# Shifting a matrix by halves with DMAs alone: which two quarters of the columns one DMA takes

## The chip, the cores and the metric

The kernel runs on one core of a Trainium2 chip. The metric is the device time of one execution in microseconds (us), and the time given for a kernel is the median over several runs. A separate execution is taken with the hardware profiler; its page and its trace are what this document reads.

A core has 16 DMA engines that move data between places in memory. The compute engines (TensorE, VectorE, ScalarE, GpSimd, which the profile calls PE, DVE, ACT and POOL) play no part in this kernel. SyncE (SP) issues the DMAs: one instruction describes a whole transfer by two access patterns, for the source and for the destination, and the transfer is then cut into packets that the DMA engines work off.

## The reference

The input is a float32 matrix of 8192 x 8192 (268 MB); the output is the same matrix shifted by half its size in both directions, cyclically:

```
def reference(x: np.ndarray) -> np.ndarray:
    return np.fft.ifftshift(x)
```

With R = C = 8192, `out[i, j] = x[(i + 4096) % 8192, (j + 4096) % 8192]`. Nothing is computed. Every element is read once and written once.

A row has 32,768 bytes. In what follows a row is thought of as four quarters of 2,048 columns (8,192 bytes), Q0 to Q3. Quarter q of an output row is quarter (q + 2) mod 4 of the input row that lies 4,096 rows away: Q0 comes from Q2, Q1 from Q3, Q2 from Q0 and Q3 from Q1.

## The kernel before, in words

Both matrices lie in the device's main memory (the profile calls it HBM; the tensors are `in_x_dram` and `out_dram`). The kernel copies straight from one to the other, with nothing in between, in a double loop (lines 37 to 42): `apart` is 4, `rows` is 16 x 4 = 64, `piece` is a quarter, 2,048 columns. The outer loop goes over 128 blocks of 64 rows. The inner loop issues two DMAs for each block, 256 in all, every one on SP's queue (`nc.sync`).

The helper `both` (lines 25 to 34) builds a DMA. Its destination pattern has three dimensions: 64 rows at a step of a row, 2 pieces at a step of half a row (`hc`), and 2,048 columns in succession. Its source pattern has the same shape, begins in the other half of the row, and steps back by half a row between the two pieces. So the first DMA of a block (`col` = 0; called A below) writes Q0 and Q2 of each of its 64 rows, reading Q2 and Q0; the second one (`col` = `piece`; called B) writes Q1 and Q3, reading Q3 and Q1. A DMA moves 64 x 2 pieces of 8,192 bytes, 1 MB.

The pieces of a DMA are spread over the 16 DMA engines, eight to each, and each engine adds a small packet that reports that its share is done. The order of the issues is the order of the loop. Nothing in the kernel waits for data; the framework gives the DMAs eight completion semaphores in rotation, so that an issue waits for the DMA that was issued eight before it.

Of the kernel before, what the change touches and what calls it, by code (L numbers as in the profile page):

```python
# [1 line left out]

# [4 lines left out]


ENGINES = 16  # L10


@with_exitstack
def kernel(
    ctx: ExitStack,
    tc: tile.TileContext,
    x: bass.AP,
    out: bass.AP,
):
    nc = tc.nc  # L20
    R, C = x.shape
    hr = R // 2
    hc = C // 2

    def both(queue, row, col, rows, piece):

        queue.dma_start(
            out=bass.AP(out.tensor, out.offset + row * C + col, [[C, rows], [hc, 2], [1, piece]]),
            in_=bass.AP(
                x.tensor,  # L30
                x.offset + (row + hr) % R * C + hc + col,
                [[C, rows], [-hc, 2], [1, piece]],
            ),
        )


    apart = 4
    piece = hc // 2
    rows = ENGINES * apart
    for row in range(0, R, rows):  # L40
        for col in (0, piece):
            both(nc.sync, row, col, rows, piece)


# [1 line left out]
_INS = ['x']  # L46
_OUTS = [((8192, 8192), 'float32')]


def kernel(**inputs):  # L50
    import numpy as _np
    import concourse.bacc as _bacc
    import concourse.tile as _tile
    from concourse import mybir as _mybir
    from concourse.bass_utils import run_bass_kernel_spmd as _run

    nc = _bacc.Bacc("TRN2", target_bir_lowering=False, num_devices=1)  # L57
    arrays, args = {}, []
    for name in _INS:
        a = _np.ascontiguousarray(inputs[name])  # L60
        if a.dtype.kind in "iu":
            a = a.astype(_np.int64)
        arrays[f"in_{name}_dram"] = a
        args.append(nc.dram_tensor(f"in_{name}_dram", a.shape, _mybir.dt.from_np(a.dtype), kind="ExternalInput").ap())
    for i, (shape, dtype) in enumerate(_OUTS):
        dt = _mybir.dt.from_np(_np.dtype(dtype))
        args.append(nc.dram_tensor(f"out_{i}_dram", shape, dt, kind="ExternalOutput").ap())
    with _tile.TileContext(nc) as tc:
        kernel(tc, *args)
    r = _run(nc, [arrays], core_ids=[0])  # L70
    got = tuple(r.results[0][f"out_{i}_dram"] for i in range(len(_OUTS)))
    return got[0]
```

## Time and profile before

| | |
|---|---|
| time, median of 3 runs (lowest, highest) | 811.06 us (810.09, 811.13) |
| the profiled execution's own time | 810.44 us |
| its span, first to last instruction | 808.7 us |
| DMAs issued, size of each | 256, 1024 KB |
| median time from issue to landing | 25.1 us |
| bytes moved by the DMA engines, mean rate | 268.47 MB, 332 GB/s |
| share of the span in which SP's DMA queue kept the 16 engines busy | 99.3% |

How to read it: the page has six parts. The first is the busy time of the engines (here only POOL's four settings of constants, 0.2 us). The second cuts the span into 40 equal slices and gives, for each, the busy share of the DMA engines in tenths (9 is 90% or more) and the rate. The third is a table of DMA queues: packets, megabytes, and the time that the packets took as a share of the span of 16 engines. The fourth is the chain of waits that ended last, the fifth lists groups of instructions, and the sixth the DMA issues by line, with the time from issue to landing. Line 27 (L27) is the `queue.dma_start` in the helper. The trace behind the page holds a record for every packet: when it started, how long it took, and how many bytes it had. "GB/s" counts a copied byte once; the line that begins with HBM counts it twice, as read and as written.

### The profile page before, as it was taken

To read this page: it belongs to the slowest core of one execution; us is meant where nothing else is said; L and a number is where in the kernel's file an instruction comes from. 1 tells how busy PE (TensorE), PEld (TensorE's weight loads), DVE (VectorE), ACT (ScalarE), POOL (GpSimd) and SP (SyncE) were. 2 spreads that over 40 slices of the span, in tenths; PEclk is the share of its full clock that TensorE was granted. 3 is DMA by queue.
4 is the path that set the end of the run, shared out by engine and by line. 5 is a ranking of instruction groups with operands and counts; after the bars stand their busy time and mean duration, and the time that the engine had idled before them with its cause. 6 is when DMAs were issued, how large, how long until landed. Compare 5 with 4: busy or idle time off the path is not lost. (4 is left out here: it accounts for less than half of the span.)

```text
span 808.7 us, 301 instructions
## 1 busy us (share of the span) xinstructions
POOL 0.2 (0%) x4
## 2 busy tenths in 40 slices
POOL 0000000000000000000000000000000000000000
DMA  8999999999999999999999999999999999999998
GB/s 301 331 335 329 336 334 330 335 332 336 332 335 334 336 331 334 339 328 335 331 335 339 334 334 337 331 336 330 336 334 331 339 332 334 333 336 331 337 335 294
DMA packets 36866, 268.47 MB, mean 332 GB/s; under 512 B 4096, under 2 KB 4096, under 8 KB 4096
## 3 DMA queue, kind: packets, MB, share of 16 engines
q1 hardware_dynamic: 36864, 268.45, 99.3%
q14 instruction: 2, 0.02, 0.0%
HBM read 268.44 MB, written 268.44 MB: 664 GB/s over the span
## 5 line engine op out<-in xcount | busy, mean ns | idle before, releaser
L57 POOL MEMSET const-bfloat16-1.0<- 128x1 bf16 x1 | 0.1, 102 | 0.0
L57 POOL MEMSET const-uint8-127<- 128x1 uint8 x1 | 0.1, 102 | 0.0
L57 POOL MEMSET const-float32-1.0<- 128x1 f32 x1 | 0.1, 99 | 0.0
L57 POOL MEMSET const-float32-0.0<- 128x1 f32 x1 | 0.1, 98 | 0.2 <-issue 0.2
## 6 DMA issues: line engine op xcount, KB each, us to landing
out_dram<-in_x_dram SPq DMA_DIRECT2D x256, 1024.0 KB, 25.1
```

What stands on the lines that cost most here:

```text
L57: nc = _bacc.Bacc("TRN2", target_bir_lowering=False, num_devices=1)
```

## The change

The helper takes the first column of each of its two pieces instead of one column and a fixed step of half a row. The loop over `col` is replaced by two calls. The number, the size and the queue of the DMAs are those of before.

```
-    def both(queue, row, col, rows, piece):
+    def two(queue, row, first, second, rows, piece):
 
+        source = (first + hc) % C
+        there = second - first
+        back = (second + hc) % C - source
         queue.dma_start(
-            out=bass.AP(out.tensor, out.offset + row * C + col, [[C, rows], [hc, 2], [1, piece]]),
+            out=bass.AP(
+                out.tensor,
+                out.offset + row * C + first,
+                [[C, rows], [there, 2], [1, piece]],
+            ),
             in_=bass.AP(
                 x.tensor,
-                x.offset + (row + hr) % R * C + hc + col,
-                [[C, rows], [-hc, 2], [1, piece]],
+                x.offset + (row + hr) % R * C + source,
+                [[C, rows], [back, 2], [1, piece]],
             ),
         )
...
     for row in range(0, R, rows):
-        for col in (0, piece):
-            both(nc.sync, row, col, rows, piece)
+        two(nc.sync, row, 0, hc + piece, rows, piece)
+        two(nc.sync, row, hc, piece, rows, piece)
```

The first DMA of a block now writes Q0 and Q3 (a step of 24 KB) and reads Q2 and Q1 (a step of 8 KB back). The second writes Q2 and Q1 (8 KB back) and reads Q0 and Q3 (24 KB forward).

## The prediction

> **What bounds the kernel now.** I read the page from its DMA parts outward, since no compute engine does anything: the queue table and the memory line first, then the 40 slices, the chain, the wait list of SP's own queue, and last the separate packet records of the trace.
>
> The queue table (queue, kind, packets, megabytes, share of sixteen engines' span) and the memory line under it:
>
> ```profile
> DMA packets 36866, 268.47 MB, mean 332 GB/s; under 512 B 4096, under 2 KB 4096, under 8 KB 4096
> ## 3 DMA queue, kind: packets, MB, share of 16 engines
> q1 hardware_dynamic: 36864, 268.45, 99.3%
> q14 instruction: 2, 0.02, 0.0%
> HBM read 268.44 MB, written 268.44 MB: 664 GB/s over the span
> ```
>
> The sixteen DMA engines are busy 99.3% of the span: there is no idle time to win, only the length of a packet. The packets are 32,768 of 8,192 bytes with data (256 DMAs x 128) and 4,096 small ones that report completion (16 for each DMA).
>
> ```profile
> DMA  8999999999999999999999999999999999999998
> GB/s 301 331 335 329 336 334 330 335 332 336 332 335 334 336 331 334 339 328 335 331 335 339 334 334 337 331 336 330 336 334 331 339 332 334 333 336 331 337 335 294
> ```
>
> The rate is flat. Between the first and the last slice it stays within 328 and 339, and those two are the ramp and the drain. There is no stage that is worse than another.
>
> The chain of waits holds nothing of use: its seven pieces end after half a microsecond with POOL's constants, so it doesn't follow the transfers. The list of waits of SP's queue does:
>
> ```profile
> engine line waited for: us in total, times, longest us
> SPq L27 <- DMA out_dram<-in_x_dram: 634.0, 248, 3.2
> SPq L68 <- DMA out_dram<-in_x_dram: 24.1, 4, 15.2
> ```
>
> and the row of the issues, by tensor:
>
> ```profile
> L27 SPq DMA_DIRECT2D out_dram<-in_x_dram x256: 562/562/682, 0.7 to 783.1; - x128
> DMA to landing us min/median/max: 6.0/25.1/26.0
> ```
>
> An issue takes SP 562 ns; 248 of the 256 issues (all but eight) first wait for an earlier DMA to land, 634.0 / 248 = 2.56 us each. 808.7 / 256 = 3.16 us pass per DMA, so a landing time of 25.1 us means eight DMAs in flight. SP is ahead of the engines throughout.
>
> What a packet costs I took from the single packet records. The 8,192-byte ones take 391.0 ns on average, the completion packets 9 ns. Check: (32,768 x 391.0 + 4,096 x 9) / 16 = 803.1 us, which is the 99.3% of 808.7. The durations have a floor: 62% of the data packets take 307 to 320 ns, the median is 309, and the other 38% reach up to 1,507. So 391.0 is 309 plus a mean stall of 82 ns. [...] That is the only thing that this change can reach. The conversion for all that follows: each engine moves 32,768 / 16 = 2,048 data packets, so **1 ns per data packet is 2.05 us**, and 0.2% of the time (1.6 us, about what a measurement of this kernel can tell from no change) is 0.8 ns per packet.
>
> **The change, part by part.** Call the four 8 KB quarters of a 32 KB row Q0 to Q3. Output quarter q always comes from input quarter q+2 (mod 4) of the row 4,096 rows away. Before, DMA A writes Q0,Q2 (reads Q2,Q0) of 64 rows and DMA B writes Q1,Q3 (reads Q3,Q1). After, A writes Q0,Q3 (reads Q2,Q1) and B writes Q2,Q1 (reads Q0,Q3).
>
> *Counts, sizes, issue.* 256 DMAs of 64 x 2 x 8 KB, one queue, one wait each: all as before; the access patterns keep their three dimensions, and one with a negative step stands in every DMA of before too (input side). So 256 x 562 ns = 144 us of SP's issue time stay, covered by the 2.56 us wait each. An issue would have to grow from 562 ns to over 3.1 us to show. Cost 0. The start (first issue at 0.7 us) and the drain (last slice at 294 GB/s) have the same DMA sizes: 0.
>
> *Packets.* The same 32,768 of 8,192 bytes. In the new order two neighbours in an engine's sequence can be contiguous in memory (Q3 of a row, then Q0 of the next), but they are separate runs of the pattern, so I count no merging. Cost 0.
>
> *Order of addresses.* This is all that is left, and the trace of before shows no run with the new order, so I bound it. I chained the packet records per engine (each next packet starts 3 to 4 ns before the end of the one before it; 3,131 sequences between two completion packets come out unambiguous, 76% of all). That gives the mean duration by place in the engine's eight packets (four rows of two pieces; I take it that the rows of an engine follow each other): 400.6, 386.2, 389.4, 398.0, 401.9, 384.7, 390.0, 401.7 ns, each +-2.6, mean 394.1. Three things are read from it.
>
> First, reads against writes. Before, every second packet of an engine reads the same row offset that the packet before it wrote, and writes the one that it read (places 1, 3, 5, 7, counting from 0). After, no quarter is both read and written within a DMA. If such meetings cost anything, odd places would be dearer than even ones. They are 393 against 395: nothing to win there.
>
> Second, mixing. Before, all packets of one DMA stand in even quarters or all in odd ones; other engines' packets are of the other kind only around a change of DMA. After, each DMA holds both kinds, half and half. The trace has this mixture at the two places beside the change of DMA (0 and 7, where 0.375 of the overlapping packets belong to another DMA), and, without it, at the two places beside the middle of a DMA (3 and 4, where that share is 0.05), which otherwise look alike, since the engines step to the next pair of rows there too. Means: 401.15 against 399.95, a difference of +1.2 +- 2.7 ns. The mixture's share there is 0.325 more; the change raises it over all packets from 0.17 (mean of the eight places) to 0.5, as much. So the direct estimate is +1.2 +- 2.7 ns, +2.5 +- 5.5 us: not told from zero.
>
> Third, the ends. Four places (1, 2, 5, 6) average 387.6, the four others 400.6: the largest effect of place on a packet that before shows, 6.5 ns to either side of the mean. If the new order made all packets like the cheap places, 6.5 x 2.05 = 13 us would go (798); if like the dear ones, 13 us would come (824). I take 0, since the two comparisons that bear on this change (393/395 and 401/400) show nothing, and keep 798 and 824 for the range.
>
> A fourth row agrees: in the first 20 us the engines run within about 1 us of each other (spread of the sixteen completions of a DMA), later within 2 to 2.5 us, so that quarters go from nearly in step to well mixed; the full slices at the start (331 335 329 336) and the end (331 337 335) are the same.
>
> Sum: 810.44 us of the profiled execution + 0 = 810.4, and the median of the three runs, 811.06, lies 0.6 above it. I forecast **811 us**, no change.
>
> A rule of the skill, beside this sum: the Trainium skill, DMA: Bandwidth & Descriptors, Latency and other measured facts, reports that copies between memory tensors slow down when parallel streams lie at large powers of two (207 GB/s at a 512 KiB pitch, 103 at 4 MiB, and 214 again with 4 KiB of padding) and infers, unverified, that lock-stepped streams fall on the same channels. The engines here step by powers of two, so by that rule breaking the common 16 KB step would help; the trace's flat rate from in-step to mixed speaks against its applying to this bit. And the Trainium skill, HBM Reference, Specifications, gives about 716 GB/s per domain: the row's 664 would be 93% of that, and 536.9 MB at 716 an estimate of 750 us, so by that page little could be won however the order is changed.
>
> **The rivals.** *Slower: the leader pays for mixed quarters.* An engine that enters a new DMA while the others are still in the old one stalls more. At place 0 with over 0.6 of its neighbours in the other DMA the mean is 453 ns; at place 4 with over 0.6 of them in the other half of the same DMA it is 432. The 20.6 ns between them, at a share of about 0.8, could be the price of meeting the other kind of quarter. Raised by 0.33 for all packets this is 8.5 ns, 17 us, 828; laggards show none of it (place 7 against place 3: both about 399), so with half of the packets leading it is 4.2 ns, 9 us: 820. Against it: the means over leaders and laggards. It decides from 0.8 ns per packet on.
>
> *Faster: reads and writes in separate quarters.* Within a DMA all reads go to two quarters and all writes to the other two. If memory keeps a quarter's rows open for one direction, packets come out like the cheap places: 387.6, 798 us. For it: cheap and dear places exist at all, so some address pattern matters. Against it: odd places read just what was written before them and are no dearer. This is also where the page's rule on pitches would lead.
>
> *The transfer changes kind:* the pattern is cut into other packets, or the rows spread over the engines otherwise. Nothing in the rows speaks for it; both patterns keep 64 rows outermost. I give it no time of its own, and 0.02 within the slower case.
>
> **How the numbers follow.** No effect of order: 0.44, of which 0.27 within 0.2%, 0.08 faster and 0.09 slower, as 0.8 ns per packet is a third of the uncertainty of my comparison. Leader pays: 0.32 at about 820 (813 to 828). Separate quarters: 0.24 at about 798 (790 to 806). So faster 0.32, within 0.2% 0.27, slower 0.41. The range 799 to 824 holds the first case (0.44), three quarters of the second (0.24) and half of the third (0.12), together 0.80; the first case's own range is 806 to 816.
>
> **What would show it.** Right: 36,864 packets on q1, DMA share about 99.3%, slices between 328 and 339, 562 ns an issue, about 25.1 us to landing, a mean data packet of 391 +- 1 ns with 62% at the floor. The slower rival: same floor, fewer packets at it, mean near 395, slices near 328, landing near 25.4. The faster one: mean near 385, slices near 338, HBM line near 674. Wrong altogether: another number of packets, or a floor that moves.

## The result and the profile after

The changed kernel takes 815.94 us (median of 9 runs, 813.66 to 820.76), the kernel before, beside it, 811.83 us (9 runs, 810.09 to 813.65). The ratio is 1.0056 with a 95% interval from 1.0031 to 1.0080: slower by about half a per cent, 4.1 us. The forecast was no change at 811; the loss lies inside the range that was given, but the interval leaves no change out.

The profiled execution is one of the longer ones, 819.08 us with a span of 817.3 us, so its own difference to the profile of before (8.6 us) is twice that of the medians. From the page of the changed kernel, the DMA parts:

```profile
GB/s 293 328 316 321 321 331 329 330 332 335 333 334 334 334 329 335 327 326 329 333 330 324 331 333 332 338 325 329 344 331 331 335 330 328 330 331 339 333 330 284
DMA packets 36866, 268.47 MB, mean 328 GB/s; under 512 B 4096, under 2 KB 4096, under 8 KB 4096
q1 hardware_dynamic: 36864, 268.45, 99.3%
HBM read 268.44 MB, written 268.44 MB: 657 GB/s over the span
out_dram<-in_x_dram SPq DMA_DIRECT2D x256, 1024.0 KB, 25.3
```

The packets are the same in number and size and the engines are as busy as before; only the rate is lower, 328 for 332 GB/s. An issue takes 573 ns instead of 562, and SP still waits before 248 of them (from the row of the issues and the wait list of the changed kernel):

```profile
L30 SPq DMA_DIRECT2D out_dram<-in_x_dram x256: 572/573/693, 0.7 to 791.8; - x128
SPq L30 <- DMA out_dram<-in_x_dram: 640.2, 248, 3.9
```

The 11 ns per issue are covered by 2.58 us of waiting each (640.2 / 248). In the packet records the mean of a data packet is 395.1 ns, for 391.0 before: 4.1 ns x 2.05 us = 8.4 us, nearly the whole difference of the two spans (8.6). The floor is where it was (median 309 ns), and more packets are at it than before, 65.9% for 61.8%. So fewer packets stall, but those that do stall longer.

Where in time it is lost, the slices show first at the beginning: 316, 321, 321 in the third to fifth, where before had 335, 329, 336. Busy time in stretches (start and end, length, POOL's busy time and count, TensorE clock, DMA share, GB/s), before:

```profile
0.00:40.00 40.00, 0.20 (x4) 1.00 0.95 316
40.00:80.00 40.00, 0.00 (x0) 1.00 1.00 331
80.00:160.00 80.00, 0.00 (x0) 1.00 1.00 334
160.00:320.00 160.00, 0.00 (x0) 1.00 1.00 335
320.00:480.00 160.00, 0.00 (x0) 1.00 1.00 334
480.00:640.00 160.00, 0.00 (x0) 1.00 1.00 334
640.00:800.00 160.00, 0.00 (x0) 1.00 1.00 334
```

and after:

```profile
0.00:40.00 40.00, 0.20 (x4) 1.00 0.95 310
40.00:80.00 40.00, 0.00 (x0) 1.00 0.99 319
80.00:160.00 80.00, 0.00 (x0) 1.00 1.00 328
160.00:320.00 160.00, 0.00 (x0) 1.00 1.00 333
320.00:480.00 160.00, 0.00 (x0) 1.00 1.00 329
480.00:640.00 160.00, 0.00 (x0) 1.00 1.00 333
640.00:800.00 160.00, 0.00 (x0) 1.00 1.00 332
```

The new order is 3.6% slower from 40 to 80 us (319 against 331) and 0.3 to 1.5% slower after 160 us. By the missing GB/s times the length of each stretch, the first 160 us hold 240 + 480 + 480 = 1,200 GB/s x us, which at 332 GB/s is 3.6 us. The 640 us after them hold 320 + 800 + 160 + 320 = 1,600, or 4.8 us. So the loss is densest at the beginning, but in this long execution more than half of it comes later. The profiles below show the first part each time, and the second not always.

### The profile page after: what moved, and what is told of

The parts are those of the page before. It is cut to its first block, busy times and chain, and to the rows that moved or that the text cites. A ratio compares the mean times of both kernels' runs of the same rounds, so it can differ in the third digit from the quotient of the medians.

```text
span 817.3 us, 301 instructions
## 1 busy us (share of the span) xinstructions
POOL 0.2 (0%) x4
## 2 busy tenths in 40 slices
DMA packets 36866, 268.47 MB, mean 328 GB/s; under 512 B 4096, under 2 KB 4096, under 8 KB 4096
```

## The experiments

All ratios are against the kernel before on the same chip; chips differ (811 us on some, 823 on one), so across chips only ratios are compared. The diffs are against the changed kernel. "Spread" below is the time from the first to the last of the sixteen completions of one DMA, and "step" the time from one DMA's median completion to the next one's, both from the landing records; they tell how far the engines stand apart and how fast they are. "Near step" means a small spread.

### Which part of the order costs

The changed kernel once more, without an edit, beside three other orders.

> The changed kernel once more, beside the kernel before on one chip, for the size of the loss and for a second profile. All theories: ratio to before near 1.005 (1.003 to 1.008). The first profile lost most in the first 80 us (310 and 319 GB/s in the two windows of 40 us, against 316 and 331 before) and about 0.7% later; if this is the change and not that one execution, the second profile shows it again: under 325 GB/s in the window from 40 to 80 us.

Measured: 825.62 us against 823.25, ratio 1.0037 (1.0021 to 1.0053). The dip is there again: 305 and 322 GB/s in the first two stretches of 40 us, 328 to 330 after. The kernel with the order turned in DMA B (below), which is as fast as before on this chip, has 312 and 329, then 328 to 329. So this profiled execution, the shortest of its nine (824.39 us), loses nothing after 80 us.

Neighbouring quarters:

```
-        two(nc.sync, row, 0, hc + piece, rows, piece)
-        two(nc.sync, row, hc, piece, rows, piece)
+        two(nc.sync, row, 0, piece, rows, piece)
+        two(nc.sync, row, hc, hc + piece, rows, piece)
```

> DMA A writes Q0,Q1 (reads Q2,Q3), DMA B writes Q2,Q3 (reads Q0,Q1): neighbours, 16 KB contiguous, ascending on both sides. As in the changed kernel, both 8 KB parities are in flight within a DMA and no quarter is both read and written. Theory 1, mixing both parities costs: slower by 0.3 to 0.8%, 814 to 818 us. Theory 2, reads and writes in separate quarters cost (or the kernel before gains by touching the same row offset for both): slower by as much. Theory 3, the descending writes of DMA B cost: no descending here, so 811 to 813, as before. Theory 4, the pairing of outer with inner quarters itself (steps of 24 and 8 KB by turns): 811 to 813.

Measured: 1.0022 (1.0009 to 1.0034). But this kernel changed something else too, as the packet line of its page shows:

```profile
DMA packets 20482, 268.47 MB, mean 326 GB/s; under 512 B 4096, under 2 KB 4096, under 8 KB 4096
```

Without the 4,096 completion packets and the two instruction packets these are 16,384 packets with data, of 16 KB: two pieces that lie in succession on both sides travel as one. So the run doesn't decide between the theories. It does have the dip (308 and 322 GB/s in the first two stretches of 40 us) without any descending order, which speaks against theory 3.

The pairs of before with the order turned in DMA B:

```
-        two(nc.sync, row, 0, hc + piece, rows, piece)
-        two(nc.sync, row, hc, piece, rows, piece)
+        two(nc.sync, row, 0, hc, rows, piece)
+        two(nc.sync, row, hc + piece, piece, rows, piece)
```

> The pairs of the kernel before, but DMA B writes Q3 first and then Q1 (reads Q1, then Q3): only the order within DMA B is turned, writes descend there. Theories 1, 2 and 4: as before, 811 to 813, ratio within 0.2%. Theory 3 (descending writes in DMA B, or turning the order from DMA to DMA): slower by 0.3 to 0.8%.

Measured: 1.0002 (0.9994 to 1.0011), as before.

The new pairs with DMA B ascending:

```
-        two(nc.sync, row, hc, piece, rows, piece)
+        two(nc.sync, row, piece, hc, rows, piece)
```

> The pairs of the changed kernel (Q0,Q3 and Q1,Q2), but DMA B writes Q1 first and then Q2, ascending (reads Q3, then Q0). Theory 3: the loss is gone, 811 to 813. Theories 1, 2 and 4: still slower by 0.3 to 0.8%, 814 to 818.

Measured: 1.0030 (1.0014 to 1.0047). Theory 3, the descending order, falls by both runs: turning alone costs nothing, and unturning doesn't help. The loss is in which quarters a DMA pairs.

Neighbours again, descending, so that they aren't merged:

```
-        two(nc.sync, row, 0, hc + piece, rows, piece)
-        two(nc.sync, row, hc, piece, rows, piece)
+        two(nc.sync, row, piece, 0, rows, piece)
+        two(nc.sync, row, hc + piece, hc, rows, piece)
```

> DMA A writes Q1 then Q0 (reads Q3, Q2), DMA B writes Q3 then Q2 (reads Q1, Q0). The earlier run with neighbours in ascending order moved 16 KB packets (16,384 of them), since the two pieces were contiguous; descending, they stay apart, 32,768 packets of 8 KB expected. So it has both parities in flight and separate quarters for reads and writes, with another pairing than the changed kernel. Theories 1 and 2 (mixing, separate quarters): slower by 0.3 to 0.5%. Theory 4 (the pairing of outer with inner quarters): as before, within 0.2%.

Measured: 816.93 us against 810.98, 1.0067 (1.0043 to 1.0091), somewhat more than the 0.3 to 0.5% expected, with 32,768 data packets of 8 KB as expected and the dip (310 and 321 GB/s, then 327, 328 and from 160 us on 333 to 335). Theory 4 falls: it is not the pairing of outer with inner quarters.

One quarter per DMA (`one` is a helper like `two` with a single piece; its definition is left out here):

```
-        two(nc.sync, row, 0, hc + piece, rows, piece)
-        two(nc.sync, row, hc, piece, rows, piece)
+        for col in (0, hc, piece, hc + piece):
+            one(nc.sync, row, col, rows, piece)
```

> One quarter per DMA: 512 DMAs of 64 x 8 KB in the order Q0, Q2, Q1, Q3, so that reads and writes stand in separate quarters within a DMA, but only one parity is in flight. It has 4,096 more completion packets (9 ns each, 2.3 us, 0.28%) and twice the issues (512 x 0.57 = 292 us, covered). Theory 1 (mixing parities): 1.003 from the completion packets alone. Theory 2 (separate quarters): 1.006 to 1.008.

Measured: 813.39 against 810.98, 1.0032 (1.0022 to 1.0042): the price of the completion packets, with no dip (its stretch from 40 to 80 us is at 334 GB/s). So reads and writes in separate quarters cost nothing by themselves. What the three slow orders with 8 KB packets (the changed kernel, DMA B ascending, neighbours descending) have in common, and the three others (before, order turned, single quarter) lack, is that a DMA touches all four quarters, even and odd ones together. Even and odd quarters together without the separation of reads and writes would need a pattern of four dimensions in one DMA and wasn't tried, so it is not shown that the mixing alone, without the separation, would cost as much.

### When it costs

The new pairs for 16 blocks only, at the beginning, and the reverse:

```
     for row in range(0, R, rows):
-        two(nc.sync, row, 0, hc + piece, rows, piece)
-        two(nc.sync, row, hc, piece, rows, piece)
+        if row < 16 * rows:
+            two(nc.sync, row, 0, hc + piece, rows, piece)
+            two(nc.sync, row, hc, piece, rows, piece)
+        else:
+            two(nc.sync, row, 0, hc, rows, piece)
+            two(nc.sync, row, piece, hc + piece, rows, piece)
```

> The new pairs for the first 16 of the 128 blocks (32 DMAs, about the first 100 us, in which the profiles of the changed kernel lose most), the pairs of before for the other 112. Theory S (the loss is in the start, while the sixteen engines run nearly in step): the whole loss remains, ratio to before 1.003 to 1.005. Theory E (every block loses the same): an eighth of it, ratio 1.0005, not told from 1.

> The reverse: the pairs of before for the first 16 blocks, the new pairs for the other 112. Theory S: no loss, ratio 0.998 to 1.001 (it could even gain, as the windows after 160 us of the second profile of the changed kernel are 1 GB/s above those of the kernel with the order turned in DMA B). Theory E: seven eighths of the loss, 1.003 to 1.004.

Measured: 1.0036 (1.0023 to 1.0049) with the new order in an eighth of the blocks, and 1.0032 (1.0020 to 1.0044) with it in the other seven eighths. Neither theory had both. The loss does not go with the number of blocks (theory E falls), and it is not tied to the beginning of the kernel (theory S falls). The stretches of the first, new until about 100 us:

```profile
40.00:80.00 40.00, 0.00 (x0) 1.00 0.99 324
80.00:120.00 40.00, 0.00 (x0) 1.00 1.00 324
120.00:160.00 40.00, 0.00 (x0) 1.00 0.99 336
```

and of the second, new from about 100 us:

```profile
40.00:80.00 40.00, 0.00 (x0) 1.00 1.00 326
80.00:120.00 40.00, 0.00 (x0) 1.00 1.00 334
120.00:160.00 40.00, 0.00 (x0) 1.00 0.99 326
160.00:320.00 160.00, 0.00 (x0) 1.00 0.99 332
```

In the first run the dip goes away together with the new order (324, then 336). In the second one the rate falls where the new order begins and recovers while it stays (326, then 332). That second dip is weak evidence by itself: the same run has one stretch of 326 with the old pairs too, from 40 to 80 us. The time is the firmer part: all five executions took 813.5 us or more, against 810.98.

Spread and step, medians and means over 16 DMAs, with the beginning of the new order marked by `>`:

```
DMAs             0-15         16-31        32-47        64-79        128-143      144-159
                 spread step  (us, ns)
before           1.1  3124    1.1  3148    1.1  3153    1.4  3125    2.1  3145    2.1  3116
changed        > 1.3  3223    1.3  3262    2.1  3161    2.7  3163    3.4  3178    3.4  3158
new first      > 1.2  3236    1.2  3256    1.3  3122    1.2  3134    1.4  3134    1.6  3152
old first        1.2  3170    1.1  3133  > 1.5  3189    1.7  3160    2.2  3136    2.2  3146
four spells    > 1.2  3193    1.3  3230    1.8  3180    2.1  3155  > 2.2  3162    2.2  3165
old half first   1.1  3108    0.9  3155    1.1  3140    1.2  3141  > 1.5  3185    1.4  3169
half new       > 1.3  3237    1.5  3233    1.7  3275    2.2  3178    -     -      -     -
changed, again > 1.2  3253    1.3  3222    1.2  3238    1.6  3178    1.9  3134    2.1  3137
```

The last four rows belong to the next experiments ("changed, again" is the changed kernel beside the staggered ones). Over the sixteen groups of the kernel before, the step lies between 3,112 and 3,172 ns, so a single value under about 3,180 tells little. What the table suggests is that the new order is slow while the engines stand within about 1.5 us of each other. It is no sharp line (3,275 at 1.7 us), and it is not the whole loss of the first profile, which had its stretch of 329 GB/s at a spread of about 3.3 us.

### Is it a time to settle, or the engines being near step

Four spells: new for blocks 0 to 31 and 64 to 95, the pairs of before for the others (`if row // (32 * rows) % 2 == 0` in the diff above). Old half first: the pairs of before for `row < R // 2`, then the new ones.

> Blocks 0 to 31 with the new pairs, 32 to 63 with those of before, 64 to 95 new, 96 to 127 before: the new order is entered twice. Theory T (a settling time: each time the new order begins, the first 32 to 64 DMAs run 1 to 3% slower, about 3 us in all, and after that the two orders run at the same rate): twice the loss, ratio 1.006 to 1.008, and a dip in the rate at the start and again at about 404 us. Theory T1 (a settling time at the start of the kernel alone, or only while the engines are within 1.5 us of each other): the loss of one entry, 1.003 to 1.004, no dip at 404 us. Theory E (every block of the new order loses the same): half of the loss of the changed kernel, 1.002.

> The first 64 blocks with the pairs of before, the other 64 with the new ones. By the switch, at about 404 us, the completions of the sixteen engines are some 2 us apart, not 1.2 as at the start. Theory T: the whole loss, 1.003 to 1.004, with the dip after the switch. Theory T1 (engines near step are what the new order can't bear): no loss, 0.999 to 1.001. Theory E: half, 1.002, with no dip.

Measured: four spells 1.0056 (1.0043 to 1.0068), old half first 1.0022 (1.0012 to 1.0031). Four spells in stretches, the new order entered again at about 404 us:

```profile
40.00:100.00 60.00, 0.00 (x0) 1.00 1.00 326
300.00:400.00 100.00, 0.00 (x0) 1.00 1.00 333
400.00:440.00 40.00, 0.00 (x0) 1.00 1.00 332
440.00:500.00 60.00, 0.00 (x0) 1.00 1.00 333
```

and old half first, entered at about 404 us for the first time:

```profile
300.00:400.00 100.00, 0.00 (x0) 1.00 1.00 334
400.00:440.00 40.00, 0.00 (x0) 1.00 1.00 329
440.00:500.00 60.00, 0.00 (x0) 1.00 1.00 329
500.00:600.00 100.00, 0.00 (x0) 1.00 1.00 332
```

The profile of four spells has no second dip, which fits T1; the time of 1.0056 is above T1's one entry, and below T's two. Old half first has a dip, which fits T, but there the spread hadn't reached the 2 us that I expected: it was 1.2 us up to the switch. Both profiles agree with a loss near step only. The times leave it undecided.

Only the first 64 blocks, with the new pairs and with those of before (`range(0, R // 2, rows)`; both leave out the lower half of the output):

> The changed kernel, but only the first 64 blocks: it leaves out the lower half of the output. To be held against the next run, which does the same with the pairs of before. Theory T: the loss is a fixed one and stays near 3 us (2 to 4) at half the length. Theory E: it halves, to 1.5 us or so.

> The kernel before, but only the first 64 blocks: it leaves out the lower half of the output. About 0.502 of the whole kernel's time, 407 us on a chip where that takes 811, as the ramp and the drain stay. The run before this one is longer by 2 to 4 us under theory T, by 1.5 us under theory E.

Measured: 415.82 us (412.73 to 418.64) against 408.58 (408.14 to 409.40), 7.2 us. Not the 2 to 4 of theory T, but certainly not the half of theory E: at half the length the loss is no smaller than over the whole matrix (4.1 us on the first chip). So most of it belongs to the time after the order begins. In the profile of this run that time is longer than in the first one: 305, 325 and 324 GB/s up to 200 us, where the half with the old pairs has 318, 333 and 333.

### Trying to set the engines apart, and bringing them back

The engines dealt apart in the first block: 48 of its 64 rows go as before, the last 16 in small DMAs of unequal length (`one` again without its definition):

```
+    level = 3 * ENGINES
+    two(nc.sync, 0, 0, hc + piece, level, piece)
+    two(nc.sync, 0, hc, piece, level, piece)
+    for quarter, some in enumerate((12, 11, 10, 9)):
+        one(nc.sync, level, quarter * piece, some, piece)
+        one(nc.sync, level + some, quarter * piece, ENGINES - some, piece)
-    for row in range(0, R, rows):
+    for row in range(rows, R, rows):
```

> The changed kernel, but in the first block the last 16 rows are dealt out in eight small DMAs of one quarter each (12 and 4 rows, 11 and 5, 10 and 6, 9 and 7), so that, if a DMA of n rows goes to the first n engines, the sixteen engines begin the second block up to 8 packets (about 3 us) apart instead of in step. All of the matrix is copied. The engine with the most work has 4 packets above the mean, some 1.5 us at the end. Theory T1 (near step is what costs): no dip, 331 to 335 GB/s in the window from 40 to 100 us, and within 1 us of the staggered kernel of before. Theory T (settling, whatever the spread): the dip remains, 319 to 327 GB/s, and the time lies 2 to 4 us above the staggered kernel of before.

> The same stagger with the pairs of before: what the stagger itself costs. Both theories: 0 to 2 us above the kernel before (ratio 1.000 to 1.0025), no dip.

> The changed kernel on the same chip as the two staggered ones, for the size of its loss there. Both theories: ratio 1.003 to 1.008, with the dip.

Measured on one chip, before at 810.58: the changed kernel 816.82, 1.0069 (1.0051 to 1.0087), with the dip (306 and 324 GB/s up to 100 us); staggered with the old pairs 812.55, 1.0019 (1.0011 to 1.0028), as expected; staggered with the new pairs 819.80, 1.0112 (1.0084 to 1.0140). The loss of the new order against the old one with the same stagger is 7.3 us. It fits neither theory: T1 had no loss, T had a dip of 100 us, and this one lasts, at least in the profiled execution, which is the longest of its six (824.45 us). New pairs, staggered:

```profile
40.00:100.00 60.00, 0.00 (x0) 1.00 1.00 327
200.00:300.00 100.00, 0.00 (x0) 1.00 1.00 327
700.00:800.00 100.00, 0.00 (x0) 1.00 1.00 330
```

Old pairs, staggered:

```profile
40.00:100.00 60.00, 0.00 (x0) 1.00 1.00 333
700.00:800.00 100.00, 0.00 (x0) 1.00 1.00 334
```

The stagger didn't do what it was meant to do. The landing records put the spread, medians of 16 DMAs, at 1.6 to 1.9 us in the first 128 whole DMAs of the new order and at 1.1 to 1.7 in those of the old, not at the 3 us of the dealing: the engines had come nearly together again by the first whole DMA (0.6 and 0.8 us). So a wide spread from the start was not tried. What the pair does show is that one threshold for the spread is not enough: with the new pairs the step stayed at 3,161 to 3,207 ns, 3,183 on average, where the spread was 1.9 to 2.2 us, while the second new spell of four spells and the changed kernel in two profiles had 3,134 to 3,167, 3,151 on average, at 1.9 to 2.2. T1 in its plain form falls by this. That two executions with the same spread have the engines in different arrangements, and that the new order minds which one, would explain it, but no record here tells one arrangement from another. The old pairs, staggered, run at 332 to 334 from 40 to 800 us.

The changed kernel beside them supports the part of T1 that is left. In this execution the spread stayed at 1.2 to 1.3 us for the first 64 DMAs, twice as long as in the first profile, and the dip lasted about twice as long too: 324 and 325 GB/s up to 200 us, 330 in the next 100 us, then 333 to 335 to the end, as fast as the old pairs. What was left to ask is whether being near step causes the dip, or only the beginning of something.

Brought back into step seven times (`seen` is a tile of 16 x 8; its two lines are left out here):

```
     for row in range(0, R, rows):
         two(nc.sync, row, 0, hc + piece, rows, piece)
         two(nc.sync, row, hc, piece, rows, piece)
+        if row // rows % 16 == 15 and row + rows < R:
+            nc.sync.dma_start(out=seen[:, :], in_=bass.AP(out.tensor, out.offset + (row + rows - 16) * C + piece, [[C, 16], [1, 8]]))
+            nc.sync.dma_start(out=bass.AP(out.tensor, out.offset + (row + rows - 16) * C + piece, [[C, 16], [1, 8]]), in_=seen[:, :])
```

> The changed kernel, but after every 16 blocks (32 DMAs) SP reads back 16 short pieces of what the last DMA wrote, and writes the same values to the same place, before it issues the next block. So the engines run empty seven times and begin in step again eight times in all. Theory P (the dip comes from the engines being in step, a bad arrangement for four quarters): each of the eight spells of about 100 us runs 1 to 3% slower than with the old order, 2 to 3 us each, together 12 to 25 us above the next run. Rival B (the dip belongs to the beginning of the kernel, or to a change of order): once 3 to 5 us, as without the drains.

> The same seven drains with the pairs of before: what the drains cost by themselves, an estimated 25 to 60 us (each one lets the engines run empty for two round trips of short DMAs and then fill up; the shortest landing time in the trace of before is 6.0 us). Theory P: the run before this one is 12 to 25 us longer; rival B: 3 to 5 us.

Measured, before at 811.24: new 835.44 (832.87 to 836.13), ratio 1.0289 (1.0272 to 1.0306); old 815.18 (813.61 to 816.45), ratio 1.0045 (1.0032 to 1.0058). The difference is 20.3 us, in the upper half of theory P; rival B had 3 to 5. My estimate of the drains' own cost, 25 to 60 us, was far too high: with the old pairs they took about 4 us. The engines did not run empty as planned, either. The trace shows the first DMA of the next block issued ahead of the read, and the second one between the read and the write, so the DMAs in flight fall from eight to one or two. In the packet records all sixteen engines stand still together at only one of the fourteen drains. That was enough to keep them near step. Stretches of the new order:

```profile
300.00:400.00 100.00, 0.00 (x0) 1.00 1.00 322
400.00:500.00 100.00, 0.00 (x0) 1.00 0.99 323
600.00:700.00 100.00, 0.00 (x0) 1.00 0.99 323
```

and of the old one:

```profile
300.00:400.00 100.00, 0.00 (x0) 1.00 1.00 332
600.00:700.00 100.00, 0.00 (x0) 1.00 1.00 333
```

The dip of the first 100 us is now the whole run. In both kernels the spread stays at 1.1 to 1.9 us to the end, where the undrained ones reach 2.4 and 3.4; away from the drains the mean step is 3,228 ns with the new pairs and 3,141 with the old, 2.8% apart (87 ns x 256 DMAs = 22 us; the two spans are 21.8 us apart). Most of it is not in the drains themselves: the mean data packet is 400.2 ns against 391.4, and 8.8 ns x 2.05 us = 18.0 us of the 21.8. So at the same spread, with the same drains, the new order is the slower one, and kept near step it stays slow.

## Why the prediction was wrong

**What bounds the kernel, the parts that stay, the conversion:** right. Packets, floor, queue share and cover of the issues came out as told, and 2.05 us per ns accounts for nearly all of the difference of the two spans. The issue was not quite "as before" (573 for 562 ns), without effect.

**Reads against writes, "nothing to win there":** right, and confirmed from the other side: single quarters, with reads and writes apart, gain nothing and lose nothing beyond their completion packets.

**Mixing, "the direct estimate is +1.2 +- 2.7 ns, +2.5 +- 5.5 us":** the measured loss of 4.1 us is 2.0 ns per packet and lies within it. I set this term to 0 because it could not be told from zero; but zero had to be within 0.8 ns, and the comparison couldn't tell that. The best value that I had was on the slow side. That it comes near is luck, though: the four places on which it rests went down in the changed kernel (401.2 to 394.3 and 399.8 to 397.7 ns), and others went up.

**The ends, "I take 0":** here the change shows in the records. Chained as in the prediction, those of the changed kernel give 1,898 unambiguous sequences, with 395, 393, 391, 385, 410, 403, 401 and 394 ns by place, each +-3. The four places that were cheap (387.6) now take 396.9 ns, the four that were dear (400.6) take 396.0. With the drains it is the same, only more: from the old pairs to the new ones the cheap places go from 380.7 to 404.7 ns, the dear ones from 407.5 to 402.1. The new order loses the cheap places. The two comparisons that set this term to 0 could not see that: they held dear places against dear ones, or averaged cheap and dear.

**The step that failed is the 0 for the order of addresses,** which measured 2.0 ns per packet by the medians. Its last support was the fourth row, "the engines run within about 1 us of each other ... later within 2 to 2.5 us, so that quarters go from nearly in step to well mixed; the full slices ... are the same". The reading is true for the old order and was carried over to the new one. The old order is indifferent to how the engines stand (near step, drifted, after the stagger, drained: 330 to 335 GB/s in every stretch of 100 us or more after the start, on the chips where it takes 811 us), the new one is not: 322 to 326 kept near step, 327 to 330 after the stagger, 329 to 335 when drifted. A trace of a kernel that is insensitive to something can't price it for one that is sensitive.

**The rivals.** "The leader pays" had the direction and most of its signs (mean near 395, landing near 25.4, HBM line below 664), but told fewer packets at the floor, and there were more; its price of 9 us was spread evenly over the run, while the measured loss is densest where the engines are near step. Nor do the places agree with it: 3 and 4, where the share of neighbours of the other kind was lowest before (0.05) and so had most to gain, went from 399.8 to 397.7 ns, not up. "Separate quarters" as a gain is refuted. The Trainium skill, DMA: Bandwidth & Descriptors, Latency and other measured facts, infers that lock-stepped streams at large powers of two collide. That being near step matters to the new order is shown here (3,228 ns per DMA kept near step, 3,151 on average at a spread of about 2 us), but the orders that broke the common 16 KB step, which I took to help by that rule, are the ones that are sensitive to it; the order that kept it is not.

**What stays open:** why an order that touches all four quarters in a DMA is slower near step than one that touches two, and whether the mixing or the separation that comes with it does it. Which addresses collide, if any do, which arrangement is a good one, and why the run after the stagger stayed slow, no run here shows. Nor is it shown why the first profile lost 4.8 us after 160 us with the engines well apart, while two other profiles of the same kernel ended without a loss, or why four spells lost more than its one dip. The times of the new order scatter twice as wide as those of the old (7.1 against 3.6 us over nine runs each), as one would expect if each run drifts into another arrangement, but that is an argument, not a measurement.

## What to carry to other kernels

When sixteen DMA engines copy without a pause, the order of addresses within one engine's sequence counts together with how the engines stand to each other; look at the first 100 us, where they are still in step, apart from the rest. A rate that is flat in one order says nothing of another order's start. And a loss of half a per cent over the whole may be 3% over an eighth of it; here it was paid again each time that the queue was nearly drained.

## What the runs showed of the hardware

- Engines that begin together stay near step at first: over the first 16 DMAs (50 us) the median spread is 1.1 to 1.4 us in every unstaggered profile with 1 MB DMAs. How fast they drift then differs from one execution to the next: 1.2 us still at 400 us in old half first, 2.1 at 150 us in the profile of the changed kernel; at the end 2.4 in the profile of before and 3.4 in that of the changed kernel.
- Two pieces of one pattern that lie in succession on both sides travel as one packet of 16 KB (16,384 instead of 32,768 data packets); the same two pieces in descending order stay apart.
- Seven near-drains of the queue (from eight DMAs in flight to one or two), each with a read back and a write, cost 4 us together with the old pairs.
- A data packet that is not stalled takes 309 ns whichever the order; 8 KB in that time is 26.5 GB/s for one engine, while the mean was 391 to 400 ns in the whole kernels that were profiled with 8 KB packets.
